# Reading the moving operands of split fp32 products from two alternating places

## The chip, the cores and the metric

The kernel runs on one core of one Trainium2 chip. The metric is the device time of one execution in microseconds. Three runs of the kernel before took 567.93, 568.34 and 568.43 us; their median is 568.34 us. A difference of some 0.2% (1.1 us) is about the least that can be told from none.

The core's engines appear in the profile as PE (TensorE matmuls), PEld (TensorE weight loads), DVE (VectorE), ACT (ScalarE), POOL (GpSimd) and SP (SyncE, which issues most DMAs). A TensorE matmul has a stationary operand, the weights, which are loaded into the array first, and a moving operand, whose columns stream through it one after another.

## The reference

The reference is a decoder trunk of two layers on one sequence of 256 tokens with a model width of 1024, all in float32:

```
for i in range(DEPTH):                       # 2 layers
    h = rmsnorm(x, norm_mix[i])
    x = x + rglru_mixer(h, ...)              # layer 0: recurrent block
    x = x + nsa_mixer(h, ...)                # layer 1: sparse attention, 16 heads
    h = rmsnorm(x, norm_ffn[i])
    u = relu(h @ w_up)                       # 1024 x 4096
    x = x + (u * u) @ w_down                 # 4096 x 1024
out = rmsnorm(x, norm_final)
```

The recurrent block projects to 2048 columns, convolves, gates (block-diagonal 256 x 256 matrices), scans along the tokens and projects back. The attention block projects to queries, six sets of keys and values, and gates, attends over compressed, selected and window keys, and projects back.

## The kernel before

Activations lie transposed: features on the 128 partitions, the 256 tokens along the free dimension, eight such chunks for a width of 1024. A weight matrix arrives in pieces of 128 x 1024 (eight 128 x 128 blocks), read in one order throughout.

For precision at a high matmul rate, each float32 operand is split in two float32r parts: a high part, which is the value rounded, and a low part, which is the difference. A product is then three matmuls: high by high, high by low, low by high. `mm3` (lines 317 to 320) issues them for one 128 x 128 weight block and one chunk of 256 token columns, into one PSUM bank. It serves all projections, both MLPs and both output projections. The weight block is the stationary operand, and the 256 activation columns (`hhl`, the split normed input; `uhl`, the split MLP hidden layer; `xbh`/`xbl`, the product of the recurrent block; `oh`/`ol`, the attention output) are the moving one. In `values` (line 993 on) it is the other way round: the activations are stationary and the weights move, in runs of 304 and 256 columns. The gates of the recurrent block (line 686), the score products (lines 1105 and 1106), the transposes (1159) and the attention's value products (1177) are not products of `mm3`.

The weight pieces are split on the device: ACT copies the high part (line 278 in the MLPs, the helper at line 326 elsewhere), and DVE subtracts to get the low part (287 and 323).

A finished bank is evicted by DVE, multiplied by the row `rs` that holds the norm's factor for each token: line 662 (convolution input), 723 (gelu branch), 778 (MLP hidden layer, with the relu), 887 (queries), 899 and 936 (keys, compressed inputs). In the MLP, ACT then squares the result twice, into a float32 `u` and into the float32r high part in `uhl` (783 and 784), and DVE writes the low part (785). Output projections and the MLP's second matmul are evicted by adding them to the residual `xt` (522). In attention, the output of `pv` is split out of its bank by the helpers at 326 (`copy`) and 323 (`diff`).

The two mixers are emitted by a planner (`Plan`): each piece of work is added with planned durations, the keys it reads and writes, and a due time; list scheduling with a few rounds of forward and backward passes gives one static order for each engine's queue. The MLPs are written out by hand: 32 hidden tiles of 24 matmuls each, then eight output tiles of 96, with `tick` placing the weight splits between them.

Of the kernel before, what the change touches and what calls it, by code (L numbers as in the profile page):

```python
# [219 lines left out]
def trunk_kernel(ctx: ExitStack, tc: tile.TileContext, x_in, vec_in, const_in, w2_in, wts, out):  # L220
# [71 lines left out]
    def later(fn):  # L292
        deferred.append(fn)
# [16 lines left out]
    def get(name, idx):  # L310
# [4 lines left out]
        return hi_t[i % NSPL], lo_t[i % NSPL]  # L315

    def mm3(ps, wh, wl, xh, xl, start, stop):
        pe.matmul(ps, wh, xh, start=start, stop=False)  # L318
        pe.matmul(ps, wh, xl, start=False, stop=False)  # L319
        pe.matmul(ps, wl, xh, start=False, stop=stop)  # L320
# [12 lines left out]
    class Section:  # L333
# [55 lines left out]
        def proj(self, name, idx, b, t, step, xs=None, xk=None):  # L389
            wh, wl, wk = self.weight(name, idx, t)  # L390
            z = self.bank((name, idx), b, zcols)
            xs, xk = xs or [(hh[:, k], hl[:, k]) for k in range(KC)], xk or hkey
            for i in range(0, 4, self.join):
                ks = range(2 * i, 2 * (i + self.join))

                def run(e, ks=ks):
                    for k in ks:
                        w = slice(k * P, (k + 1) * P)
                        mm3(z(), wh[:, w], wl[:, w], xs[k][0], xs[k][1], k == 0, k == KC - 1)
                self.add("pe", 0.68 * self.join, run, r=wk + list(xk[ks.start:ks.stop]), w=[("ps", b)], t=t + i * step)  # L400
            return z, ("ps", b)
# [72 lines left out]
    hhl = hpool.tile([P, KC, 2, S], F32R, name="hhl")  # L474
    hh, hl = hhl[:, :, 0], hhl[:, :, 1]
    acc = spool.tile([P, S], F32, name="acc")
    rs = spool.tile([P, S], F32, name="rstd")
# [47 lines left out]
    with ExitStack() as ph:  # L525
# [100 lines left out]
        xbh_b, xbl_b = (rg.tile([P, 8, S], F32R, name=n) for n in ("xbh", "xbl"))  # L626
        xb, r_t, i_t, y_t, t_t, xbh, xbl = ([x[:, m] for m in range(8)] for x in (xb_b, r_b, i_b, y_b, t_b, xbh_b, xbl_b))
        pair = lambda x, m: x[:, m // 2 * 2:m // 2 * 2 + 2]
# [15 lines left out]
        def conv(m, t):  # L644
            b = nextbank()
            if m < NFINE:
                wh, wl, _ = sec.weight("in", 8 + m, t)
                z, zk = sec.bank(("in", 8 + m), b, zcols), ("ps", b)
                for k in range(KC):
                    def run(e, k=k):  # L650
                        w = slice(k * P, (k + 1) * P)
                        mm3(z(), wh[:, w], wl[:, w], hh[:, k], hl[:, k], k == 0, k == KC - 1)
                        if m == 0 and k == 1:
                            keep_warm(8)
                    add("pe", 0.323 + 0.9 * (m == 0 and k == 1), run, r=[("hi0", m, k // 2), ("lo0", m, k // 2), ("hi", m), ("lo", m), hkey[k]],
                        w=[zk], t=m * 0.33 + k * NI * PJ / 2 if m < NI else t + k * PJ / 2)
            else:
                z, zk = sec.proj("in", 8 + m, b, t, PJ)
            t += 4 * PJ
            x, xk = xps[m % 3], ("xp", m % 3)  # L660
            bk = ("xb", m)
            add("dve", 0.34, lambda e: e.tensor_tensor(x[:, 3:], z(), rs, op=OP.mult), r=[zk, "rs"], w=[xk], t=t)
            add("act", 0.49, lambda e: e.activation(xb[m], x[:, 3:], AF.Identity, bias=col(V_CB, m), scale=cw(3, m)),
                r=[xk], w=[bk], t=t)
            for i in range(3):
                add("dve", 0.4, lambda e, i=i: e.scalar_tensor_tensor(xb[m], x[:, i:i + S], cw(i, m), xb[m], op0=OP.mult,
                                                                      op1=OP.add), r=[xk], w=[bk], t=t)
# [53 lines left out]
        def branch(m, t):  # L721
            z, zk = sec.proj("in", m, nextbank(), t, PJ)
            add("dve", 0.34, lambda e: e.tensor_tensor(y_t[m], z(), rs, op=OP.mult), r=[zk, "rs"], w=[("y", m)], t=t + 2.6)

        def product(m, t):
            yk, hk, lk = keys("y", m), keys("xbh", m), keys("xbl", m)
            y, h, l_, x = (pair(z, m) for z in (y_b, xbh_b, xbl_b, t_b))
            add("act", 0.53, lambda e: e.activation(y, y, AF.Gelu_apprx_tanh), r=["tab"], w=yk, t=t)
            add("dve", 0.6, lambda e: e.tensor_tensor(y, y, x, op=OP.mult), r=keys("t", m), w=yk, t=t)
            add(HI2, copy(h, y), r=yk, w=hk, t=t)  # L730
            add("dve", 0.6, diff(l_, y, h), r=yk + hk, w=lk, t=t)

# [33 lines left out]
    def mlp(layer, epilogue, first, last=None):  # L766
        with ExitStack() as ph:
# [4 lines left out]
            uhl = [up.tile([P, 2 * S], F32R, name="uhl", tag="uhl", bufs=NF) for _ in range(NF)]  # L772
            uh, ul = [x[:, :S] for x in uhl], [x[:, S:] for x in uhl]
            zrot = rotation(3, 4, 5, 0, 1, 2)

            def up_post(m, z):
                t = tmp.tile([P, S], F32, name="t", tag="t")
                dve.scalar_tensor_tensor(t, z, 0.0, rs, op0=OP.max, op1=OP.mult)  # L778
                flush()
                if m >= len(first) - 1:  # L780
                    tick(n=2 if m < 16 else 1)
                u = tmp.tile([P, S], F32, name="u", tag="u")
                act.activation(u, t, AF.Square)  # L783
                act.activation(uh[m], t, AF.Square)  # L784
                later(lambda: dve.tensor_tensor(ul[m], u, uh[m].bitcast(F32), op=OP.subtract))  # L785

            for m in range(NF):
                if m >= len(first):
                    z = next(zrot)[:, :S]
                    wh, wl = get("up%d" % layer, m)  # L790
                    for k in range(KC):
                        w = slice(k * P, (k + 1) * P)
                        mm3(z, wh[:, w], wl[:, w], hh[:, k], hl[:, k], k == 0, k == KC - 1)
                else:
                    z = first[m]()
                up_post(m, z)
# [29 lines left out]
    with ExitStack() as ph:  # L826
# [27 lines left out]
        oht, olt = (at.tile([P, 8 * S], F32R, name=n) for n in ("oh", "ol"))  # L854
        oh, ol = ([x[:, i * S:(i + 1) * S] for i in range(8)] for x in (oht, olt))
        NPT_ = 16
# [24 lines left out]
        def qchunk(c, b, t, step):  # L881
# [4 lines left out]
            ak, bk = ("sa", c % NQ), ("sb", c % NQ)  # L886
            add("dve", 0.4, lambda e: e.scalar_tensor_tensor(x, z(), cst[:, C_QS + c:C_QS + c + 1], rs,
                                                             op0=OP.mult, op1=OP.mult), r=[zk, "rs"], w=[xk], t=t)
# [6 lines left out]
        def kchunk(gp, br, b, t, step):  # L895
            z, zk = proj_t(("ks", "kw")[br], gp, b, t, step)
            t += 4 * step
            x, xk, l_, lk = turn()
            add("dve", 0.34, lambda e: e.tensor_tensor(x, z(), rs, op=OP.mult), r=[zk, "rs"], w=[xk], t=t)
            x, l_ = two_blocks(x), two_blocks(l_)  # L900
# [31 lines left out]
        def cproj(i, gp, b, t, step):  # L932
            z, zk = proj_t(("ck", "cv")[i], gp, b, t, step)
            t += 4 * step
            x, xk, _, _ = turn()
            add("dve", 0.34, lambda e: e.tensor_tensor(x, z(), rs, op=OP.mult), r=[zk, "rs"], w=[xk], t=t)
            for hf in range(2):
# [60 lines left out]
        def values(t):  # L998
# [3 lines left out]
            for i in range(4):  # L1002
                wh, wl, wk = weight("v", i, t + 2.8 * i)
                for kk in range(2):
                    k = 2 * i + kk
                    for h in range(2):
                        def run(e, wh=wh, wl=wl, k=k, kk=kk, h=h):
                            ts_ = slice(h * P, (h + 1) * P)
                            for b, c0 in enumerate((0, S + 48)):
                                ws = slice(kk * NVCOL + c0, kk * NVCOL + c0 + ncol[b])  # L1010
                                ps = vz[h][b]()
                                e.matmul(ps, hh[:, k, ts_], wh[:, ws], start=(k == 0), stop=False)  # L1012
                                e.matmul(ps, hh[:, k, ts_], wl[:, ws], start=False, stop=False)  # L1013
                                e.matmul(ps, hl[:, k, ts_], wh[:, ws], start=False, stop=(k == KC - 1))  # L1014
                        add("pe", 0.77, run, r=wk + [hkey[k]], w=[("ps", banks[h][0]), ("ps", banks[h][1])],
# [153 lines left out]
        def pv(js, t):  # L1169
            bk, n = [("ps", 7)], len(js)  # L1170
            o = zview(("o", js[0]), 7, lambda x: x[:, :n * S])
            cols = slice(js[0] * S, (js[-1] + 1) * S)

            def run(e):
# [14 lines left out]
            ok, lk = ([(x, j) for j in js] for x in ("oh", "ol"))  # L1189
            add([("act", 0.1 + 0.24 * n, 0.0), ("dve", 0.07 + 0.27 * n, 0.2)], lambda e: copy(oht[:, cols], o())(e), r=bk, w=ok,  # L1190
                t=t + 1.9 * n)
            add("dve", 0.07 + 0.27 * n, lambda e: diff(olt[:, cols], o(), oht[:, cols])(e), r=bk + ok, w=lk, t=t + 1.9 * n + 0.3)

# [115 lines left out]
def _arrange(inp):  # L1309
# [26 lines left out]
    kv = lambda i: win[:, D + i * S:D + (i + 1) * S]  # L1336
    wv = np.concatenate([kv(3), win[:, D + 6 * S:], kv(5)], axis=1).reshape(KC, P, NVCOL)
    wo = f["nsa_w_out"][0]
# [72 lines left out]
```

## Time and profile before

| | |
|---|---|
| median of three runs | 568.34 us |
| span of the profiled execution, first to last instruction | 566.4 us |
| median of the runs less that span | 1.9 us |
| mean granted TensorE clock | 0.997 |
| PE busy | 559.3 us, 4902 records |
| DVE busy | 407.6 us, 873 instructions |
| ACT busy | 343.9 us, 670 instructions |
| moved by DMA | 103.66 MB, mean 183 GB/s |

The profile shows one execution; its span stands for its own time, and the runs' times hold some 2 us more around it. Busy times of matmul records overlap: a record lasts longer than the distance to the next record's start, so the cost of a matmul is read from the distance of starts, or from counts in a window. In the views, a line such as "L318 PE MATMUL bank<-hhl,whi 128*128 128x256 f32" is line 318 of the kernel, on TensorE, writing `bank` from `hhl` and `whi`, with a 128 x 128 stationary operand and 256 moving columns.

### The profile page before, as it was taken

How to read it: one execution, taken by the hardware profiler on the slowest of the kernel's cores; microseconds unless marked ns; L12 is line 12 of the kernel's file. 1: busy time of each engine (PE TensorE's matmuls, PEld its weight loads, DVE VectorE, ACT ScalarE, POOL GpSimd, SP SyncE). 2: the span in 40 equal slices, each digit the busy share in tenths (PEclk: the TensorE clock that was granted, in tenths of full speed). 3: DMA queues.
4: the chain of work that ended last, by engine and by line, in shares of the span. 5: the costliest groups of instructions: out<-in, count | busy, mean ns of one | idle time of the engine just before them, and what ended most of it. 6: DMA issues, size and time to landing. Idle time of an engine off the chain costs nothing.

```text
span 566.4 us, 12406 instructions
## 1 busy us (share of the span) xinstructions
PE 559.3 (99%) x4902; PEld 552.9 (98%) x4902; DVE 407.6 (72%) x873; ACT 343.9 (61%) x670; POOL 40.1 (7%) x55
## 2 busy tenths in 40 slices
PE   9999999999999999999999999999999999999995
PEld 9989999999999999999999999999999999999995
DVE  6899989776676565466839999999767775563532
ACT  7699675866564443354647999875855664443421
POOL 1000000000000121131000000000000000222310
PEclk9999999999999999999999999999999999999998
DMA  8936467566667456555765431264766667566402
GB/s 319 407 91 220 117 219 247 176 204 192 188 192 249 155 189 217 190 181 175 276 188 166 140 99 57 75 224 138 221 200 192 196 200 233 154 202 221 132 1 74
DMA packets 33225, 103.66 MB, mean 183 GB/s; under 512 B 3856, under 2 KB 8080, under 8 KB 33168
## 3 DMA queue, kind: packets, MB, share of 16 engines
q1 hardware_dynamic: 32624, 102.42, 56.1%
q8 instruction: 38, 0.62, 0.5%
q10 hardware_dynamic: 544, 0.46, 0.2%
q14 instruction: 19, 0.16, 0.1%
HBM read 99.23 MB, written 1.05 MB: 177 GB/s over the span
## 4 chain that ended last, share of the span: by engine, by line
PE 99%; DVE 0%; ACT 0%; DVEq 0%; POOL 0%; issue 0%; POOLq 0%
PE bank L318 28%; PE bank L319 28%; PE bank L320 28%; PE bank L1177 3%; PE bank L686 2%; PE bank L1159 2%; PE bank L1105 1%; PE bank L1106 1%; PE bank L567 1%; PE bank L1012 1%; PE bank L1013 1%; PE bank L1014 1%; PE bank L953 1%; DVE xg L1295 0%; PE bank L1287 0%; DVEq L1406 0%
## 5 line engine op out<-in xcount | busy, mean ns | idle before, releaser
L318 PE MATMUL bank<-hhl,whi 128*128 128x256 f32 x768 | 213.1, 278 | 0.0
L319 PE MATMUL bank<-hhl,whi 128*128 128x256 f32 x768 | 212.4, 277 | 0.0
L320 PE MATMUL bank<-hhl,wlo 128*128 128x256 f32 x768 | 212.3, 276 | 0.0
L318 PEld LDWEIGHTS bank<-hhl,whi 128*128 128x128 f32 x768 | 144.5, 188 | 0.1
L287 DVE TENSOR_TENSOR wlo<-raw,whi 128x1024 fp32r<-128x1024 f32 x115 | 143.2, 1266 | 1.9 <-ACT whi L278 1.9
L319 PEld LDWEIGHTS bank<-hhl,whi 128*128 128x128 f32 x768 | 144.5, 188 | 0.1
L320 PEld LDWEIGHTS bank<-hhl,wlo 128*128 128x128 f32 x768 | 144.4, 188 | 0.0
L319 PE MATMUL bank<-uhl,whi 128*128 128x256 f32 x512 | 141.4, 276 | 0.0
L320 PE MATMUL bank<-uhl,wlo 128*128 128x256 f32 x512 | 141.3, 276 | 0.0
L318 PE MATMUL bank<-uhl,whi 128*128 128x256 f32 x512 | 141.3, 276 | 0.0
L278 ACT CAST whi<-raw 128x1024 fp32r<-128x1024 f32 x116 | 118.1, 1039 | 23.1 <-issue 18.8
L318 PEld LDWEIGHTS bank<-uhl,whi 128*128 128x128 f32 x512 | 96.1, 188 | 0.0
L320 PEld LDWEIGHTS bank<-uhl,wlo 128*128 128x128 f32 x512 | 96.1, 188 | 0.0
L319 PEld LDWEIGHTS bank<-uhl,whi 128*128 128x128 f32 x512 | 96.1, 188 | 0.0
L323 DVE TENSOR_TENSOR wlo<-raw,whi 128x1024 fp32r<-128x1024 f32 (+2 forms) x72 | 77.1, 1089 | 2.9 <-ACT whi L326 2.8
L326 ACT CAST whi<-raw 128x1024 fp32r<-128x1024 f32 (+2 forms) x64 | 61.2, 969 | 16.8 <-PE bank L319 7.8
L522 DVE TENSOR_TENSOR xt<-xt,bank 128x256 f32<-128x256 f32 x39 | 15.9, 417 | 74.8 <-PE bank L320 74.5
L783 ACT ACTIVATE u<-t 128x256 f32<-128x256 f32 x64 | 26.7, 418 | 58.6 <-DVE t L778 57.2
L778 DVE SCALAR_TENSOR_TENSOR t<-bank,rstd 128x256 f32<-128x256 f32 x64 | 26.9, 423 | 41.0 <-PE bank L320 40.7
L1119 ACT ACTIVATE pt<-pt,mx 128x128 f32<-128x128 f32 (+1 forms) x64 | 28.6, 450 | 1.8 <-DVE mx L1116 1.4
L785 DVE TENSOR_TENSOR uhl<-u,uhl 128x256 fp32r<-128x256 f32 x64 | 26.6, 416 | 3.0 <-ACT uhl L784 3.0
L498 ACT ACTIVATE hhl<-xt,vec 128x256 fp32r<-128x256 f32 x8 | 4.1, 510 | 39.4 <-DVE xt L522 39.4
(202 smaller groups left out, 732.6 us busy)
## 6 DMA issues: line engine op xcount, KB each, us to landing
raw<-in_dram SPq DMA_DIRECT2D x171, 512.0 KB, 4.4
raw<-in_dram SPq DMA_DIRECT2D x4, 560.0 KB, 4.6
gw<-in_dram SPq DMA_DIRECT2D x4, 512.0 KB, 8.9
raw<-in_dram SPq DMA_DIRECT2D x6, 256.0 KB, 4.9
y<-in_dram SPq DMA_DIRECT2D x2, 512.0 KB, 7.4
pT<-in_dram SPq DMA_DIRECT2D x2, 512.0 KB, 5.4
xt<-in_dram SPq DMA_DIRECT2D x3, 256.0 KB, 4.9
kl<-tl SPq DMA_DIRECT2D x8, 64.0 KB, 4.0
```

The costliest lines, as they stand in the source:

```text
L278: (act.copy if eng is None else eng.tensor_copy)(hi_t[i % NSPL][:, :n], raw_of(i)[:, :n])
L287: (eng or dve).tensor_tensor(lo[:, :n], raw_of(i)[:, :n], hi[:, :n].bitcast(F32), op=OP.subtract)
L318: pe.matmul(ps, wh, xh, start=start, stop=False)
L319: pe.matmul(ps, wh, xl, start=False, stop=False)
L320: pe.matmul(ps, wl, xh, start=False, stop=stop)
L323: return lambda e: e.tensor_tensor(o, a, h.bitcast(F32), op=OP.subtract)
L326: return lambda e: (e.copy if e is act else e.tensor_copy)(o, a)
L778: dve.scalar_tensor_tensor(t, z, 0.0, rs, op0=OP.max, op1=OP.mult)
L783: act.activation(u, t, AF.Square)
L785: later(lambda: dve.tensor_tensor(ul[m], u, uh[m].bitcast(F32), op=OP.subtract))
L1119: add("act", (0.39, 0.49)[qc], lambda e, row=row, j=j: e.activation(row, row, AF.Exp, bias=mx[:, j:j + 1], scale=-1.0, accum_out=sm[:, j:j ...
L1177: two = lambda c, w, y, **k: [e.matmul(o()[own_(hf), c0 + c.start:c0 + c.stop], w(hf), y(hf), **k) for hf in range(2)]
```

## The change

Three small helpers make views of a tile. `walk` shows 256 columns in the order 0, 128, 1, 129, ..., as pairs of columns 128 apart; `walks` does so for each chunk of a tile of several chunks; `pairs` shows columns in their plain order, two by two, so that its shape fits the others.

- In `mm3`, the destination in PSUM is viewed as `pairs`, which leaves its order as it was, and every caller hands in the moving operand as a `walk` view. The 256 columns of one matmul are thus read in turn from the first and the second half of the chunk.
- Where the moving operand holds tokens in their plain order (`hhl`), the result in PSUM has the tokens interleaved (token 0, 128, 1, ...). The eviction undoes it: it reads PSUM in order and writes its tile through `walk`, and reads `rs` through `walk`.
- Where the moving operand is itself written on the device for a later product (`uhl`, `xbh`/`xbl`, `oh`/`ol`), it is written through the `walk` view, so that the alternating read returns the tokens in plain order, and the residual addition at line 522 stays as it is.
- In `values`, the moving weights are read as `walk` views, for runs of 304 and 256 columns (152 and 128 apart), and the host stores these weight columns halved (all even ones, then all odd ones), so that the result comes out in plain order.

The number of instructions, their sizes, the planned durations and the DMAs are the same. The score products, gates, transposes and statistics keep their operands as they were.

```diff
+    def pairs(x):
+        return x.rearrange("p (a i) -> p a i", i=2)
+
+    def walk(x):
+        return x.rearrange("p (i a) -> p a i", i=2)
+
+    def walks(x):
+        return x.rearrange("p k (i a) -> p k a i", i=2)
+
     def mm3(ps, wh, wl, xh, xl, start, stop):
+        ps = pairs(ps)
         pe.matmul(ps, wh, xh, start=start, stop=False)
         pe.matmul(ps, wh, xl, start=False, stop=False)
         pe.matmul(ps, wl, xh, start=False, stop=stop)
...
-            xs, xk = xs or [(hh[:, k], hl[:, k]) for k in range(KC)], xk or hkey
+            xs, xk = xs or [(hhw[:, k], hlw[:, k]) for k in range(KC)], xk or hkey
...
     hh, hl = hhl[:, :, 0], hhl[:, :, 1]
+    hhw, hlw = walks(hh), walks(hl)
...
+        xbhw, xblw = walks(xbh_b), walks(xbl_b)
...
-            add("dve", 0.34, lambda e: e.tensor_tensor(x[:, 3:], z(), rs, op=OP.mult), r=[zk, "rs"], w=[xk], t=t)
+            add("dve", 0.34, lambda e: e.tensor_tensor(walk(x[:, 3:]), pairs(z()), walk(rs), op=OP.mult), r=[zk, "rs"], w=[xk], t=t)
...
-            y, h, l_, x = (pair(z, m) for z in (y_b, xbh_b, xbl_b, t_b))
+            y, h, l_, x = (pair(z, m) for z in (y_b, xbhw, xblw, t_b))
+            yw = y.rearrange("p k (a i) -> p k a i", i=2)
...
-            add(HI2, copy(h, y), r=yk, w=hk, t=t)
-            add("dve", 0.6, diff(l_, y, h), r=yk + hk, w=lk, t=t)
+            add(HI2, copy(h, yw), r=yk, w=hk, t=t)
+            add("dve", 0.6, diff(l_, yw, h), r=yk + hk, w=lk, t=t)
...
-            uh, ul = [x[:, :S] for x in uhl], [x[:, S:] for x in uhl]
+            uh, ul = [walk(x[:, :S]) for x in uhl], [walk(x[:, S:]) for x in uhl]
...
-                dve.scalar_tensor_tensor(t, z, 0.0, rs, op0=OP.max, op1=OP.mult)
+                dve.scalar_tensor_tensor(walk(t), pairs(z), 0.0, walk(rs), op0=OP.max, op1=OP.mult)
...
-                act.activation(uh[m], t, AF.Square)
-                later(lambda: dve.tensor_tensor(ul[m], u, uh[m].bitcast(F32), op=OP.subtract))
+                act.activation(uh[m], pairs(t), AF.Square)
+                later(lambda: dve.tensor_tensor(ul[m], pairs(u), uh[m].bitcast(F32), op=OP.subtract))
...
-                                ps = vz[h][b]()
-                                e.matmul(ps, hh[:, k, ts_], wh[:, ws], start=(k == 0), stop=False)
-                                e.matmul(ps, hh[:, k, ts_], wl[:, ws], start=False, stop=False)
-                                e.matmul(ps, hl[:, k, ts_], wh[:, ws], start=False, stop=(k == KC - 1))
+                                ps = pairs(vz[h][b]())
+                                e.matmul(ps, hh[:, k, ts_], walk(wh[:, ws]), start=(k == 0), stop=False)
+                                e.matmul(ps, hh[:, k, ts_], walk(wl[:, ws]), start=False, stop=False)
+                                e.matmul(ps, hl[:, k, ts_], walk(wh[:, ws]), start=False, stop=(k == KC - 1))
...
-            add([("act", 0.1 + 0.24 * n, 0.0), ("dve", 0.07 + 0.27 * n, 0.2)], lambda e: copy(oht[:, cols], o())(e), r=bk, w=ok,
+            add([("act", 0.1 + 0.24 * n, 0.0), ("dve", 0.07 + 0.27 * n, 0.2)], lambda e: copy(ohw[:, oj], ow())(e), r=bk, w=ok,
...
-            add("dve", 0.07 + 0.27 * n, lambda e: diff(olt[:, cols], o(), oht[:, cols])(e), r=bk + ok, w=lk, t=t + 1.9 * n + 0.3)
+            add("dve", 0.07 + 0.27 * n, lambda e: diff(olw[:, oj], ow(), ohw[:, oj])(e), r=bk + ok, w=lk, t=t + 1.9 * n + 0.3)
...
-    wv = np.concatenate([kv(3), win[:, D + 6 * S:], kv(5)], axis=1).reshape(KC, P, NVCOL)
+    halved = lambda w: w.reshape(D, -1, 2).transpose(0, 2, 1).reshape(D, -1)
+    wv = np.concatenate([kv(3), win[:, D + 6 * S:]], axis=1), kv(5)
+    wv = np.concatenate([halved(w) for w in wv], axis=1).reshape(KC, P, NVCOL)
```

The other evictions (lines 723, 887, 899 and 936), the attention output `oh`/`ol` and the callers of `mm3` are changed in the same manner.

More of the change, by code (lines that the diff above doesn't have):

```diff
@@ L626, in trunk_kernel @@
         xbh_b, xbl_b = (rg.tile([P, 8, S], F32R, name=n) for n in ("xbh", "xbl"))
-        xb, r_t, i_t, y_t, t_t, xbh, xbl = ([x[:, m] for m in range(8)] for x in (xb_b, r_b, i_b, y_b, t_b, xbh_b, xbl_b))
+        xbhw, xblw = walks(xbh_b), walks(xbl_b)
+        xb, r_t, i_t, y_t, t_t, xbh, xbl = ([x[:, m] for m in range(8)] for x in (xb_b, r_b, i_b, y_b, t_b, xbhw, xblw))
         pair = lambda x, m: x[:, m // 2 * 2:m // 2 * 2 + 2]
@@ L651, in run @@
                         w = slice(k * P, (k + 1) * P)
-                        mm3(z(), wh[:, w], wl[:, w], hh[:, k], hl[:, k], k == 0, k == KC - 1)
+                        mm3(z(), wh[:, w], wl[:, w], hhw[:, k], hlw[:, k], k == 0, k == KC - 1)
                         if m == 0 and k == 1:
@@ L722, in branch @@
             z, zk = sec.proj("in", m, nextbank(), t, PJ)
-            add("dve", 0.34, lambda e: e.tensor_tensor(y_t[m], z(), rs, op=OP.mult), r=[zk, "rs"], w=[("y", m)], t=t + 2.6)
+            add("dve", 0.34, lambda e: e.tensor_tensor(walk(y_t[m]), pairs(z()), walk(rs), op=OP.mult), r=[zk, "rs"], w=[("y", m)], t=t + 2.6)
         def product(m, t):
             yk, hk, lk = keys("y", m), keys("xbh", m), keys("xbl", m)
-            y, h, l_, x = (pair(z, m) for z in (y_b, xbh_b, xbl_b, t_b))
+            y, h, l_, x = (pair(z, m) for z in (y_b, xbhw, xblw, t_b))
+            yw = y.rearrange("p k (a i) -> p k a i", i=2)
             add("act", 0.53, lambda e: e.activation(y, y, AF.Gelu_apprx_tanh), r=["tab"], w=yk, t=t)
             add("dve", 0.6, lambda e: e.tensor_tensor(y, y, x, op=OP.mult), r=keys("t", m), w=yk, t=t)
-            add(HI2, copy(h, y), r=yk, w=hk, t=t)
-            add("dve", 0.6, diff(l_, y, h), r=yk + hk, w=lk, t=t)
+            add(HI2, copy(h, yw), r=yk, w=hk, t=t)
+            add("dve", 0.6, diff(l_, yw, h), r=yk + hk, w=lk, t=t)
         at_ = {}
@@ L792, in mlp @@
                         w = slice(k * P, (k + 1) * P)
-                        mm3(z, wh[:, w], wl[:, w], hh[:, k], hl[:, k], k == 0, k == KC - 1)
+                        mm3(z, wh[:, w], wl[:, w], hhw[:, k], hlw[:, k], k == 0, k == KC - 1)
                 else:
@@ L854, in trunk_kernel @@
         oht, olt = (at.tile([P, 8 * S], F32R, name=n) for n in ("oh", "ol"))
-        oh, ol = ([x[:, i * S:(i + 1) * S] for i in range(8)] for x in (oht, olt))
+        ohw, olw = (walks(x.rearrange("p (k s) -> p k s", s=S)) for x in (oht, olt))
+        oh, ol = ([x[:, i] for i in range(8)] for x in (ohw, olw))
         NPT_ = 16
@@ L886, in qchunk @@
             ak, bk = ("sa", c % NQ), ("sb", c % NQ)
-            add("dve", 0.4, lambda e: e.scalar_tensor_tensor(x, z(), cst[:, C_QS + c:C_QS + c + 1], rs,
+            add("dve", 0.4, lambda e: e.scalar_tensor_tensor(walk(x), pairs(z()), cst[:, C_QS + c:C_QS + c + 1], walk(rs),
                                                              op0=OP.mult, op1=OP.mult), r=[zk, "rs"], w=[xk], t=t)
@@ L898, in kchunk @@
             x, xk, l_, lk = turn()
-            add("dve", 0.34, lambda e: e.tensor_tensor(x, z(), rs, op=OP.mult), r=[zk, "rs"], w=[xk], t=t)
+            add("dve", 0.34, lambda e, x=x: e.tensor_tensor(walk(x), pairs(z()), walk(rs), op=OP.mult), r=[zk, "rs"], w=[xk], t=t)
             x, l_ = two_blocks(x), two_blocks(l_)
@@ L935, in cproj @@
             x, xk, _, _ = turn()
-            add("dve", 0.34, lambda e: e.tensor_tensor(x, z(), rs, op=OP.mult), r=[zk, "rs"], w=[xk], t=t)
+            add("dve", 0.34, lambda e, x=x: e.tensor_tensor(walk(x), pairs(z()), walk(rs), op=OP.mult), r=[zk, "rs"], w=[xk], t=t)
             for hf in range(2):
@@ L1171, in pv @@
             o = zview(("o", js[0]), 7, lambda x: x[:, :n * S])
-            cols = slice(js[0] * S, (js[-1] + 1) * S)
+            oj = slice(js[0], js[-1] + 1)
+            ow = lambda: o().rearrange("p (k a i) -> p k a i", k=n, i=2)
             def run(e):
```

## The prediction

> **What bounds the kernel now.** I read the page's busy shares and the chain of waits first, then what TensorE waits for.
>
> ```profile
> span 566.4 us, 12406 instructions
> PE 559.3 (99%) x4902; PEld 552.9 (98%) x4902; DVE 407.6 (72%) x873; ACT 343.9 (61%) x670; POOL 40.1 (7%) x55
> PE 99%; DVE 0%; ACT 0%; DVEq 0%; POOL 0%; issue 0%; POOLq 0%
> PE bank L567 <- POOL warm L562: 1.3, 1, 1.3
> PE bank L1281 <- ACT sqh L1278: 0.3, 1, 0.3
> ```
>
> TensorE is busy for 99% of the span, the chain that ends last is TensorE for 99%, and it waited for other engines for 1.6 us in all. So time can only move through what a matmul costs, unless another engine becomes too slow to feed it. Busy time does not say what a matmul costs, because records overlap: each lasts about 0.28 us and the next starts much earlier. The spacing of starts is the price. Here is the order of time in the first MLP:
>
> ```profile
> 120.15 0.28 PE L320 MATMUL bank<-hhl,wlo 128*128 128x256 f32 x1
> 120.27 0.28 PE L318 MATMUL bank<-hhl,whi 128*128 128x256 f32 x1
> 120.38 0.28 PE L319 MATMUL bank<-hhl,whi 128*128 128x256 f32 x1
> 120.49 0.28 PE L320 MATMUL bank<-hhl,wlo 128*128 128x256 f32 x1
> ```
>
> Three products of `mm3` take 0.34 us, 113 ns each. Two long stretches by window (columns: length, then busy time and count of PE, weight loads, DVE, ACT, POOL; granted clock; DMA share; GB/s) give it finely:
>
> ```profile
> 95.00:165.00 70.00, 70.00 (x620) 70.00 (x619) 50.91 (x82) 43.98 (x83) 0.00 (x0) 1.00 0.64 199
> 190.00:260.00 70.00, 70.00 (x620) 70.00 (x619) 38.87 (x38) 27.45 (x31) 14.01 (x12) 1.00 0.60 198
> ```
>
> 620 counted in 70 us, or about 618 spacings (records that only reach over an edge are counted too), is 113.3 ns. It is the same in both windows at a granted clock of 1.00, though DVE is busy 51 us in one and 39 in the other, and ACT 44 and 27. So the spacing is set inside TensorE and its own operand reads, not by the other engines' traffic.
>
> **Is 113.3 ns all array time?** Other matmuls of this trace say no. From the chain in order of time (start, length, count):
>
> ```profile
> 29.64 12.95 PE bank L686 x60
> 331.86 0.66 PE bank L1159 x6
> 284.14 3.62 PE bank L953 x64
> ```
>
> L686 (the gates) multiplies plain fp32: 60 records of 256 columns in 12.95 us, 215.8 ns each. L1159 (the transposes) takes 0.66/6 = 110 ns for 128 columns. Both draw a column about every 0.84 ns, with a weight load for each. `mm3` draws columns about twice as fast. Half of a gate record is 107.9 ns for 256 columns; the transpose, with the same number of 0.42 ns slots, is 110. I take 109 ns, an estimate between these, as what 256 columns would cost if drawing them at the double rate added nothing. So 113.3 holds about 4.3 ns that appears only at the double rate. Other split products pay more, in the value projection, where the weights are the moving operand, and for a while in the query projection:
>
> ```profile
> 280.53 0.28 PE L1012 MATMUL bank<-whi,hhl 128*128 128x256 f32 x1
> 280.89 0.30 PE L1012 MATMUL bank<-whi,hhl 128*128 128x304 f32 x1
> 281.31 0.28 PE L1012 MATMUL bank<-whi,hhl 128*128 128x256 f32 x1
> 281.66 0.30 PE L1012 MATMUL bank<-whi,hhl 128*128 128x304 f32 x1
> ```
> ```profile
> 333.10 0.28 PE L318 MATMUL bank<-hhl,whi 128*128 128x256 f32 x1
> 333.46 0.28 PE L318 MATMUL bank<-hhl,whi 128*128 128x256 f32 x1
> 333.81 0.28 PE L318 MATMUL bank<-hhl,whi 128*128 128x256 f32 x1
> ```
>
> Three 256-column products of `values` take 0.35 to 0.36 us, 117 to 120 ns each; three of 304 columns take 0.42, 140 ns. The second fence shows the very instructions of `mm3` at 0.71/6 = 118 ns. So the extra is not a constant of the instruction: it goes with how the two operand streams of TensorE, the moving columns and the weights of the next product, meet. What comes from where, and when, matters, and that is what the change alters.
>
> **The change part by part.**
>
> *Reading the moving operand* (`mm3`, `values`). No instruction is added or taken away, and planned durations and queue orders stay as they are: SP and POOL are not touched. Only the order of the addresses changes: column 0, 128, 1, 129 and so on in place of 0, 1, 2, 3. Counts by line in the two long stretches:
>
> ```profile
> 45.00:265.00 220.00, 178.18 (x646) 121.18 (x646) 1.00 0.60 194
> 375.00:560.00 185.00, 148.19 (x537) 100.66 (x537) 1.00 0.55 172
> ```
>
> These are the rows of L318; L319 and L320 alternate with it one for one, so they hold 3 x (646 + 537) = 3549 products at 113.3 ns. No row of this trace has this address pattern at the double rate, so its price is bounded from both sides. The low end is 107.9 ns (half a gate record): 3549 x 5.4 = 19.2 us saved. The high end comes from L953, whose moving columns lie 16 elements apart: 62 columns in 3.62/64 = 56.6 ns a record, and, since it writes the two halves of the array in turn, up to 113 ns a pair. That is 0.9 to 1.8 ns per scattered column, and it allows anything up to a fourfold spacing. Between ends so far apart I take 109 ns: the extra shows only where neighbouring columns are drawn at the double rate from one contiguous run, that run is what the change ends, and L953 shows scattered columns, at the half rate, running within a few per cent of the gates' 0.84 ns if its two halves run one after the other. Saved: 3549 x 4.3 = 15.3 us.
>
> [...]
>
> The remaining 192 + 307 + 166 = 665 products of `mm3` lie in the loading phase and the attention:
>
> ```profile
> 5.00:30.00 25.00, 18.14 (x64) 12.30 (x64) 1.00 0.98 381
> 265.00:330.00 65.00, 28.30 (x102) 18.98 (x101) 1.00 0.58 182
> 330.00:375.00 45.00, 15.67 (x56) 10.47 (x56) 1.00 0.31 90
> ```
>
> At 4.3 ns they would give 2.9 us. I count half, 1.5, because the first stretch is set by transfers too (DMA share 0.98) and DVE is nearly full in the attention. `values` has 96 products: 48 of 256 columns at about 118 ns and 48 of 304 at 140. At 109, and 109 x 304/256 = 129, they save 48 x 9 + 48 x 11 = 1.0 us.
>
> *The evictions and splits that now write or read with a step of 128.* Their count does not change. DVE rows:
>
> ```profile
> L323 DVE TENSOR_TENSOR wlo<-raw,whi 128x1024 fp32r<-128x1024 f32 x56 | 67.4, 1216 | 2.8 <-ACT whi L326 2.8
> L323 DVE TENSOR_TENSOR wlo<-raw,whi 128x256 fp32r<-128x256 f32 x12 | 4.6, 419 | 0.0
> L778 DVE SCALAR_TENSOR_TENSOR t<-bank,rstd 128x256 f32<-128x256 f32 x64 | 26.9, 423 | 41.0 <-PE bank L320 40.7
> L785 DVE TENSOR_TENSOR uhl<-u,uhl 128x256 fp32r<-128x256 f32 x64 | 26.6, 416 | 3.0 <-ACT uhl L784 3.0
> ```
>
> Two-input DVE work goes at (1216 - 419)/768 = 1.04 ns per element. If each stepped element cost a second such slot, an eviction of 256 columns would go from 0.42 to 0.69 us. The cover, by stage:
>
> ```profile
> 20.00:60.00 40.00, 40.00 (x296) 38.35 (x297) 38.92 (x80) 38.00 (x70) 2.17 (x7) 1.00 0.56 196
> 60.00:170.00 110.00, 110.00 (x971) 110.00 (x970) 87.55 (x143) 70.45 (x125) 0.00 (x0) 1.00 0.64 198
> 310.00:375.00 65.00, 65.00 (x622) 61.41 (x622) 63.07 (x326) 59.14 (x191) 0.00 (x0) 1.00 0.34 99
> 375.00:470.00 95.00, 95.00 (x841) 95.00 (x840) 72.84 (x123) 63.03 (x117) 0.00 (x0) 1.00 0.63 199
> ```
>
> Each MLP has 32 of L778 and 32 of L785, so 64 x 0.27 = 17 us more in the worst case, against 22 us of DVE idle time in each of those stages: hidden. In 20 to 60 DVE has only 1.1 us to spare against at most 16 projection evictions, 4.3 us; in 310 to 375 it has 1.9 us against 9 evictions and 4 double-length differences, 4.6 us. Without cover that is up to 3.2 + 2.7 = 6 us, and the next matmul to want the bank is what would be late. The low end is nothing: one element per slot whatever its address. A gain is excluded, as no element is left out. I take 1 us, near the low end, since these rows show DVE issuing at its plain one-element pace, without a faster mode that a step could switch off. ACT's stepped writes (the squares, the attention copies) have 40, 32 and 6 us of idle time in these stages.
>
> *The host's reordering of the value weights* changes no transfer size and no device work: nothing.
>
> **Sum.** -15.3 - 1.5 - 1.0 + 1 = -16.8 us on a span of 566.4, so 549.6. The runs' median of 568.34 is 1.9 us above the profiled span, which I leave as it is: 551.5 us. Everything behind a matmul follows it, and at 4% less per product the feeds still fit: one weight piece serves 24 products, now 2.72 us and then 2.62, against 1.22 us on DVE for the low part.
>
> **The rivals.**
>
> *The read order is indifferent.* The extra belongs to the weight stream, or to a rhythm of issue, and 113.3 stays. For it: the extreme regularity, 618 spacings per 70 us in stages of very different load. Against it: transposes and gates load weights too and show no such extra. Time: 568.3, up to 570 with some DVE cost.
>
> *The good rhythm is lost* (the other side). `mm3` at 113.3 is the best of the double-rate rows; the other rows at 256 columns stand at 117 to 120. If alternating reads meet the weight reads the way those do, every product costs about 118: 3549 x 4.7 = +16.7 us, and 585. It decides as soon as the spacing exceeds 113.3 by more than 0.3 ns, which is 1.1 us. For it: the same instructions do run at 118 in the query projection. Against it: the weights as moving operand are one contiguous run as well, so contiguity does not protect.
>
> *One fetch per column.* If a fetch serves several neighbouring columns at the double rate, an alternating read needs one per column and falls to the half rate that the gates show, 215.8 ns: 3549 x 102.5 = +364 us in the long stretches, and about +68 for the other 665 products: 1000 us. For it: every row at the double rate here reads a contiguous run, and the scattered one is at the half rate. Against it: nothing measured. [...]
>
> **How the numbers follow.** Chances: the forecast 0.62, indifferent 0.13, lost rhythm 0.14, one fetch per column 0.11. The forecast's own range is 548 (107.9 ns) to 560 (half the extra stays, or DVE's 6 us come out). The wide range must leave out at most 0.2: 548 to 586 takes in the first three and leaves out the last and the edges. A change within 0.2% (1.1 us) can't be told from none. Faster 0.62; the same 0.13; slower 0.14 + 0.11 = 0.25.
>
> **What would show it.** Right: starts of L318 to L320 at 109 ns, about 642 counted in a 70 us MLP window in place of 620; the value projection at 109 and 129; L778 and L785 near 0.42 us. Indifferent: 620 again. Lost rhythm: about 595. One fetch per column: about 326. If L778 or L785 stand at 0.69 us, the evictions cost what I set aside, and waits of PE for DVE should appear between 310 and 375. I am wrong if the spacing does not fall, or if TensorE starts to wait.

## The result, and the profile after

The changed kernel takes 565.1 us (median of four runs, 564.78 to 565.2) against 568.25 us before (four runs). The ratio is 0.9943, 95% interval 0.9929 to 0.9958: faster by 0.6%, about 3.2 us. The prediction was 551.5 us.

The page of the changed kernel, first lines and chain (before, TensorE held 99% of the chain):

```profile
span 563.4 us, 12407 instructions
PE 553.3 (98%) x4902; PEld 544.9 (97%) x4902; DVE 429.6 (76%) x873; ACT 358.0 (64%) x670; POOL 40.2 (7%) x55
PE 78%; DVE 15%; DMA 3%; ACT 2%; issue 1%; SPq 1%; POOL 0%; DVEq 0%; ACTq 0%; POOLq 0%
```

The span is 3.0 us shorter. TensorE is busy 6.0 us less, so 3.0 us of idle time are new, and DVE now holds 15% of the chain. DVE is busy 22.0 us more and ACT 14.1 us more with the same number of instructions. The two windows inside the first MLP (length, then busy time and count of PE, weight loads, DVE, ACT, POOL; granted clock, DMA share, GB/s):

```profile
95.00:165.00 70.00, 70.00 (x629) 70.00 (x628) 59.06 (x84) 49.93 (x83) 0.00 (x0) 1.00 0.65 203
190.00:260.00 70.00, 70.00 (x629) 70.00 (x628) 39.37 (x38) 27.46 (x31) 13.98 (x12) 1.00 0.61 203
```

Some 627 spacings in 70 us are 111.6 ns, where 618 were 113.3. By the trace's starts, taken to the nanosecond, 600 products in a row of the MLP average 111.67 ns, and 113.33 before; I write 111.7 from here on. The read did become faster, by 1.7 ns a product, not by 4.3. The value projection went near to where it was expected, from 140 and 118 ns to about 130 and 111 (129 and 109 were predicted). Its order of time:

```profile
289.78 0.29 PE L1027 MATMUL bank<-wlo,hhl 128*128 128x304 f32 x1
289.91 0.29 PE L1028 MATMUL bank<-whi,hhl 128*128 128x304 f32 x1
290.04 0.27 PE L1026 MATMUL bank<-whi,hhl 128*128 128x256 f32 x1
290.15 0.28 PE L1027 MATMUL bank<-wlo,hhl 128*128 128x256 f32 x1
290.26 0.28 PE L1028 MATMUL bank<-whi,hhl 128*128 128x256 f32 x1
290.38 0.29 PE L1026 MATMUL bank<-whi,hhl 128*128 128x304 f32 x1
```

290.04 less 289.78 is 0.26 us for two products of 304 columns; 290.38 less 290.04 is 0.34 us for three of 256. To the nanosecond, the starts lie 132, 129 and 129 ns apart for three of 304 and then 109, 112 and 112 for three of 256, over and over.

The groups of the stepped evictions and of the low part of the recurrent block's product (`xbl`; its row before stands last), and the waits of TensorE (line numbers are those of the changed file: 791, 797 and 798 were 778, 784 and 785; 333 was 323):

```profile
L791 DVE SCALAR_TENSOR_TENSOR t<-bank,rstd 128x256 f32<-128x256 f32 x64 | 39.4, 620 | 22.7 <-PE bank L330 22.6
L798 DVE TENSOR_TENSOR uhl<-u,uhl 128x256 fp32r<-128x256 f32 x64 | 40.9, 639 | 2.8 <-ACT uhl L797 2.8
L797 ACT ACTIVATE uhl<-t 128x256 fp32r<-128x256 f32 x64 | 42.5, 664 | 0.0
L333 DVE TENSOR_TENSOR xbl<-y,xbh 128x512 fp32r<-128x512 f32 x4 | 4.4, 1103 | 0.1
L323 DVE TENSOR_TENSOR xbl<-y,xbh 128x512 fp32r<-128x512 f32 x4 | 2.7, 673 | 0.0
```
```profile
PE bank L329 <- DVE xbl L333: 1.2, 2, 1.0
PE bank L329 <- DVE ol L333: 0.7, 1, 0.7
PE bank L328 <- ACT xbh L336: 0.4, 1, 0.4
```

A stepped eviction on DVE went from 0.42 to 0.62 to 0.64 us, ACT's stepped square from 0.40 to 0.66 us, and a low part of 512 columns from 0.67 to 1.10 us. TensorE now waits for `xbl` and for the low part of the attention output (`ol`), which it did not before.

### The profile page after: what moved, and what is told of

The parts are those of the page before. It is cut to its first block, busy times and chain, and to the rows that moved or that the text cites. A ratio compares the mean times of both kernels' runs of the same rounds, so it can differ in the third digit from the quotient of the medians.

```text
span 563.4 us, 12407 instructions
## 1 busy us (share of the span) xinstructions
PE 553.3 (98%) x4902; PEld 544.9 (97%) x4902; DVE 429.6 (76%) x873; ACT 358.0 (64%) x670; POOL 40.2 (7%) x55
## 4 chain that ended last, share of the span: by engine, by line
PE 78%; DVE 15%; DMA 3%; ACT 2%; issue 1%; SPq 1%; POOL 0%; DVEq 0%; ACTq 0%; POOLq 0%
PE bank L329 24%; PE bank L328 23%; PE bank L330 23%; DVE wlo L333 3%; DMA raw<-in_dram 2%; PE bank L1192 2%; DVE xb L678 1%; DVE pt L1130 1%; PE bank L1173 1%; DVE pt L1158 1%; DVE t L730 1%; SPq L547 1%; PE bank L1026 1%; PE bank L1027 1%; PE bank L1028 1%
## 5 line engine op out<-in xcount | busy, mean ns | idle before, releaser
L328 PEld LDWEIGHTS bank<-hhl,whi 128*128 128x128 f32 x768 | 147.7, 192 | 0.4 <-DVE tt L950 0.3
L330 PEld LDWEIGHTS bank<-hhl,wlo 128*128 128x128 f32 x768 | 147.7, 192 | 0.0
L329 PEld LDWEIGHTS bank<-hhl,whi 128*128 128x128 f32 x768 | 147.7, 192 | 0.0
L278 ACT CAST whi<-raw 128x1024 fp32r<-128x1024 f32 x116 | 120.2, 1057 | 21.1 <-issue 17.9
L329 PEld LDWEIGHTS bank<-uhl,whi 128*128 128x128 f32 x512 | 98.3, 192 | 0.0
L330 PEld LDWEIGHTS bank<-uhl,wlo 128*128 128x128 f32 x512 | 98.3, 192 | 0.0
L328 PEld LDWEIGHTS bank<-uhl,whi 128*128 128x128 f32 x512 | 98.3, 192 | 0.0
L791 DVE SCALAR_TENSOR_TENSOR t<-bank,rstd 128x256 f32<-128x256 f32 x64 | 39.4, 620 | 22.7 <-PE bank L330 22.6
L798 DVE TENSOR_TENSOR uhl<-u,uhl 128x256 fp32r<-128x256 f32 x64 | 40.9, 639 | 2.8 <-ACT uhl L797 2.8
L797 ACT ACTIVATE uhl<-t 128x256 fp32r<-128x256 f32 x64 | 42.5, 664 | 0.0
```

What stands on the lines that cost most here:

```text
L278: (act.copy if eng is None else eng.tensor_copy)(hi_t[i % NSPL][:, :n], raw_of(i)[:, :n])
L791: dve.scalar_tensor_tensor(walk(t), pairs(z), 0.0, walk(rs), op0=OP.max, op1=OP.mult)
L797: act.activation(uh[m], pairs(t), AF.Square)
L798: later(lambda: dve.tensor_tensor(ul[m], pairs(u), uh[m].bitcast(F32), op=OP.subtract))
```

## The experiments

Theory A: the alternating read saves what the spacing shows, and the stepped evictions give a good part of it back. Rival B: the evictions are harmless, and the new waits come only from TensorE running ahead.

### The read alone

```diff
 def mm3(ps, wh, wl, xh, xl, start, stop):
+    ps, xh, xl = seq(ps), alt(xh), alt(xl)   # alt: 0, 128, 1, 129, ...
```

`values` reads its weights the same way; nothing else changes, so results come out in another order.

> The kernel before with the alternating read alone: mm3 and values read their moving operand through walk, and every eviction, split and host layout stays as it was (so tokens and value columns come out interleaved where they should not). Theory A (the read saves 1.7 ns per product, from 113.3 to 111.7 ns, and the stepped evictions of the full change give about half of it back in waits): spacing 111.7 ns, values at 109 to 112 and 129 ns, DVE and ACT rows as before, no new waits of PE; 4224 x 1.65 ns + 0.8 us saved, about 560.5 us. Rival B (the waits seen after the change come from TensorE being faster, not from the evictions): 565 us, with the same waits.

Measured: 559.83 us, ratio 0.9857 (0.9843 to 0.9872). In the windows view:

```profile
95.00:165.00 70.00, 70.00 (x629) 70.00 (x629) 51.42 (x84) 44.47 (x84) 0.00 (x0) 1.00 0.64 201
190.00:260.00 70.00, 70.00 (x630) 70.00 (x629) 38.81 (x40) 27.79 (x32) 15.72 (x18) 1.00 0.59 196
```

The spacing is that of the full change with DVE and ACT loaded as before, and the waits for `xbl` and `ol` are gone (TensorE's waits come to 1.8 us, with 1.6 before). The read is worth 568.0 - 559.8 = 8.2 us. Rival B falls: TensorE is just as fast here and does not wait for either.

### The stepped evictions alone

```diff
 def mm3(ps, wh, wl, xh, xl, start, stop):
-    ps = pairs(ps)
+    ps = halves(ps)                       # plain order again:
+    xh, xl = xh.rearrange("p a i -> p i a"), xl.rearrange("p a i -> p i a")
```

`values` reads in plain order again too.

> The changed kernel with contiguous reads in mm3 and values, so that only the stepped evictions and splits are left (the tokens are then in a wrong order). Theory A: spacing 113.3 ns as before, L778/L785-like rows at 0.62 and 0.64 us, waits of PE around the recurrent block's product and in the attention; 2 to 4 us slower than before, 570 to 572 us. Rival B: no waits, 568 us.

Measured: 573.35 us, ratio 1.0092 (1.0075 to 1.0109), 5.4 us slower. The two largest new waits are those of the changed kernel, though the spacing is the old one:

```profile
PE bank L332 <- DVE xbl L336: 1.2, 2, 1.0
PE bank L332 <- DVE ol L336: 0.7, 1, 0.7
```
```profile
190.00:260.00 70.00, 70.00 (x620) 70.00 (x619) 41.39 (x40) 29.33 (x33) 14.12 (x13) 1.00 0.59 195
```

These waits sum to 1.9 us only, as they count moments when no matmul is in flight. The starts show the whole loss: set matmul by matmul beside the kernel before, this run falls behind by 0.2 us in the first 45 us, 2.3 us in the recurrent block's product, 0.3 us near 280 us and 1.8 us between 330 and 381 us, 4.7 us in all in the profiled executions. Between these places, in both MLPs, it loses nothing.

So -8.2 for the read and +5.4 for the evictions make -2.8 us, against -3.2 measured for both. That is where the gain went. A and B differed on this run too, and it went A's way, at more than A's 2 to 4 us.

### The same evictions with the loops swapped

```diff
-dve.scalar_tensor_tensor(walk(t), pairs(z), 0.0, walk(rs), ...)      # p a i: destination steps 512 bytes
+dve.scalar_tensor_tensor(halves(t), evens(z), 0.0, halves(rs), ...)  # p i a: source steps 8 bytes
```

Every stepped eviction and split is done so; which element goes where is unchanged.

> The changed kernel with the loops of every stepped eviction and split swapped: the destination in SBUF is written in its plain order (first half, then second half), and the source, PSUM or SBUF, is read with a step of two columns (8 bytes). Same result, same number of instructions. Theory A with the step of 512 bytes as the cause of the dear evictions: the rows return from 0.62-0.66 us to about 0.42 us, the waits go, 561 us. Rival: any step costs the same on DVE and ACT: rows stay at 0.62 us or more, 565 us.

Measured: 559.97 us, ratio 0.9859 (0.9843 to 0.9876), equal to the read alone. The groups:

```profile
L803 DVE SCALAR_TENSOR_TENSOR t<-bank,rstd 128x256 f32<-128x256 f32 x64 | 26.8, 421 | 37.1 <-PE bank L342 36.8
L810 DVE TENSOR_TENSOR uhl<-u,uhl 128x256 fp32r<-128x256 f32 x64 | 27.7, 432 | 3.3 <-ACT uhl L809 3.3
L809 ACT ACTIVATE uhl<-t 128x256 fp32r<-128x256 f32 x64 | 31.0, 485 | 0.0
```

The waits for `xbl` and `ol` are gone again. It was the step of 512 bytes in SBUF that cost, not stepping as such: a PSUM source read at every second column costs DVE nothing (0.42 us), an SBUF source 0.02 us on DVE and 0.08 on ACT. On ACT only the write had the long step. On DVE a second operand in SBUF was read with it as well, and no run separates that from the write. This kernel computes the same thing as the kernels before and after the change, and is faster than both.

### What bounds the product at 111.7 ns?

In the value projection after the change, 304 columns take about 129 ns, and that is 109 ns worth for 256. So the moving side can probably go faster than 111.7, and something else seems to hold `mm3`. Theory C: the load of 128 weight columns. Rival D: a rest of the moving side's extra. The edit is made to the kernel with swapped loops (559.97 us), and it leaves out 32 of the 128 output rows in every product that neither starts nor ends its group:

```diff
+    if not (start or stop):
+        ps, wh, wl = ps[:96], wh[:, :96], wl[:, :96]
```

> The kernel with swapped loops, in which every product of mm3 that neither starts nor ends its group loads only 96 of its 128 weight columns and writes 96 partitions; the work of the other 32 output rows is left out there. The 256 moving columns and their order stay. Theory C (at 111.7 ns the weight load of 128 columns is what bounds a product, the alternating read itself needs only 109): such products fall to 109 ns, in the MLP's second matmul nearly all of them; about 642 counted per 70 us there; about 552 us. Rival D (111.7 is what is left of the moving side's extra): spacing stays at 111.7 and the time at 560 us.

Measured, in one run beside one of before (568.08): 552.36 us. Windows, and a load of each size from the groups:

```profile
190.00:260.00 70.00, 70.00 (x642) 70.00 (x641) 41.89 (x44) 29.53 (x35) 16.32 (x18) 1.00 0.58 191
```
```profile
L342 PEld LDWEIGHTS bank<-uhl,whi 128*96 128x96 f32 x481 | 78.3, 163 | 0.0
L343 PEld LDWEIGHTS bank<-hhl,whi 128*128 128x128 f32 x192 | 36.8, 192 | 0.0
```

About 640 spacings in 70 us are 109.4 ns. With the moving operand untouched and a quarter fewer weight columns, the product falls to the 109 ns of the prediction, and D falls. The edit also writes a quarter fewer rows of PSUM, which by itself would leave a rival. The value projection of the changed kernel answers it, with all 128 columns and rows: of its three products of 256 columns, the first takes 109 ns and the next two 112. The first comes behind three of 304 columns, at 129 ns each, and its load starts 127 ns ahead of it; the loads of the next two start 107 and 109 ns ahead. (Why the first product of 304 takes 132 stays open.) So 109 ns is measured twice, with a smaller load and, at full size, where the load had started earlier. Both fit C; that at 111.7 ns the weight load is late is my reading of them.

### Can the weight load gain in the same way?

An alternating order of the stationary columns was not run. (From here on, a line is a name for addresses: an aligned group of 16 bytes, four columns.) Two plain steps were run, on the kernel with swapped loops, with the blocks woven on the host to keep the result:

```diff
+def block(w, k):
+    return w[:, :D].rearrange("p (j k) -> p k j", k=8)[:, k]       # step 32 bytes
+    # second run: pairs of blocks woven, step 8 bytes
```

> The kernel with swapped loops, in which the 128 columns of each weight block of mm3 are read with a step of 8 columns (32 bytes); the host weaves the blocks of a piece so that the result is the same. The first three pieces and the value weights keep their layout. If the weight load bounds at 111.7 ns and its extra comes, as on the moving side, from reading a contiguous run: 109 ns and about 550 us. [...] If it does not care: 111.7 ns and 560 us.

> The kernel with swapped loops, in which two neighbouring weight blocks of mm3 are woven column by column on the host and each is read with a step of 2 columns (8 bytes), two columns of every 16-byte line; same result; first three pieces and value weights as they were. If the weight load, which bounds at 111.7 ns, gains from touching each line less often in a row: down to 109 ns and 550 us. [...] If it does not care: 111.7 ns, 560 us.

Measured, one run each: 1090.41 us for 32 bytes (before: 568.08) and 591.07 us for 8 bytes (before: 567.82). The window of 95 to 165 us in each:

```profile
95.00:165.00 70.00, 70.00 (x293) 70.00 (x293) 31.14 (x49) 22.16 (x35) 0.00 (x0) 1.00 0.33 106
```
```profile
95.00:165.00 70.00, 70.00 (x589) 70.00 (x588) 49.02 (x78) 44.21 (x78) 0.00 (x0) 1.00 0.55 188
```

That is 240 and 119 ns a product, or 1.9 and 0.93 ns per weight column, against 0.87 contiguous. Of the three forms the contiguous block is the best, so 111.7 stands for 128 x 128 blocks until a better one is found. The product became dearer (240 and 119 ns against 111.7) with only the reading of its weights changed, as C says.

### What is it about the read order?

The first attempt was a read order that needs no change elsewhere, because PSUM is written in the same jumping order:

```diff
+    ps, xh, xl = walk(ps), walk(xh), walk(xl)   # "p (i b c) -> p b i c", i=2, c=2: runs of two
```

> The kernel before, with mm3 and values reading two neighbouring columns from the first half, then two from the second half, and so on, and writing them to PSUM in the same jumping order, so that the result lies in plain order and no eviction and no layout changes. Theory A, if runs of two columns are enough to take the extra off the read and PSUM takes jumps between runs of 8 bytes at full rate: 111.7 ns, 560.5 us. Rival (jumps in PSUM cost time, or runs of two keep the extra): 113.3 ns and 568 us, or a larger spacing and over 570 us.

Measured: 800.13 us, ratio 1.4086 (1.4065 to 1.4107). Its two parts alone:

> The kernel before, with mm3 and values reading runs of two neighbouring columns in turn from the first and the second half (0, 1, 128, 129, 2, 3), and PSUM written in plain order; evictions as before, so tokens and value columns come out in another order. It is the earlier run with jumps in PSUM (800 us) without the jumps. If PSUM's jumps made that one slow: 111.7 to 113.3 ns, 560 to 568 us. If the read of runs of two made it slow: about 167 ns and 800 us.

> The kernel before, with mm3 and values reading their moving columns in plain order and writing PSUM in jumping order, runs of two columns in turn to the first and the second half; evictions as before, so tokens and value columns come out in another order. If PSUM's jumps made the earlier run slow: about 167 ns and 800 us. If not: 113.3 ns and 568 us.

Measured: 799.93 us for the read of runs of two, 568.12 us for the jumps in PSUM (before: 567.82). The window of each, in this order:

```profile
95.00:165.00 70.00, 70.00 (x421) 70.00 (x420) 38.33 (x64) 32.33 (x58) 0.00 (x0) 1.00 0.36 122
```
```profile
95.00:165.00 70.00, 70.00 (x620) 70.00 (x619) 50.89 (x82) 44.24 (x83) 0.00 (x0) 1.00 0.60 199
```

167 ns against 113.3: it is the read, and PSUM takes jumps between runs of two columns for nothing. Reading 0, 1, 128, 129 takes half as long again as 0, 128, 1, 129. So more orders were read, by `mm3` alone (each as a comment with its view; the fourth and the fifth belong to the test at the end of this section):

```diff
+# 0, 16, 32, ... 240, 1, 17, ...    "p (q r) -> p r q", r=16
+# 0, 4, 1, 5, 2, 6, 3, 7, 8, 12     "p (b i a) -> p b a i", i=2, a=4
+# 0, 2, 1, 3, 4, 6, 5, 7            "p (b i a) -> p b a i", i=2, a=2
+# 0, 128, 2, 130, ... 1, 129, 3     "p (i a b) -> p b a i", i=2, b=2
+# 0, 64, 128, 192, 1, 65, ...       "p (i a) -> p a i", i=4
```

> The kernel before, with mm3 reading its 256 moving columns in turn from sixteen places 16 columns (64 bytes) apart: 0, 16, 32 and so on, then 1, 17; PSUM is written in order and evictions are as before, so tokens come out in another order; values is as before. If any read that leaves the 16-byte line at every column is as good as two places: 111.7 ns, 561 us. [...]

> The kernel before, with mm3 reading in turn from two places only 4 columns (16 bytes) apart: 0, 4, 1, 5, 2, 6, 3, 7, then 8, 12 and so on; PSUM in order, evictions as before, tokens in another order, values as before. If alternating between two neighbouring 16-byte lines is enough: 111.7 ns, 561 us. If the two places must lie far apart: 113.3 ns or more, 568 us or more.

> The kernel before, with mm3 reading its moving columns as 0, 2, 1, 3, then 4, 6, 5, 7: in turn from two places 2 columns (8 bytes) apart, within one 16-byte line; PSUM in order, evictions as before, tokens in another order, values as before. If what helps is that neighbouring columns come from two different lines: no gain, 113.3 ns and 568 us. If any break of the plain order helps: 111.7 ns, 561 us.

One run each. Sixteen places: 1018.68 us (before: 568.08). Two places 16 bytes apart: 560.85 us (568.08). Two places 8 bytes apart: 567.92 us (567.82). Their windows, in this order:

```profile
95.00:165.00 70.00, 70.00 (x321) 65.61 (x320) 33.23 (x52) 24.29 (x38) 0.00 (x0) 1.00 0.37 117
```
```profile
95.00:165.00 70.00, 70.00 (x630) 70.00 (x629) 51.43 (x84) 44.40 (x83) 0.00 (x0) 1.00 0.65 203
```
```profile
95.00:165.00 70.00, 70.00 (x620) 70.00 (x619) 50.89 (x82) 44.36 (x83) 0.00 (x0) 1.00 0.58 199
```

219, 111.7 and 113.3 ns. The distance of 128 columns is not needed, two neighbouring lines do. One count sorts all of these: take the even places of the order and the odd places apart, and count how many columns in a row of each lie in one line. In plain order there are two (0, 2, then 4, 6); alternating between two lines, four; alternating within a line, two; with runs of two or sixteen places, one. Two last orders set this count against the simpler rule that neighbours must come from different places (Model N):

> The kernel before, with mm3 reading in turn from two places 128 columns apart, but in each of them first all even columns, then all odd ones: 0, 128, 2, 130, 4, 132, and later 1, 129, 3, 131. PSUM in order, evictions as before, tokens in another order, values as before. [...] Model N (it is enough that neighbours in the order come from two different places): 111.7 ns and 561 us.

> The kernel before, with mm3 reading in turn from four places 64 columns apart: 0, 64, 128, 192, 1, 65 and so on. PSUM in order, evictions as before, tokens in another order, values as before. [...] Model N: 111.7 ns, 561 us.

Measured: 568.34 us for the first (before: 568.65) and 680.44 us for the second. Windows, in this order:

```profile
95.00:165.00 70.00, 70.00 (x620) 70.00 (x619) 50.91 (x82) 44.02 (x83) 0.00 (x0) 1.00 0.63 198
```
```profile
95.00:165.00 70.00, 70.00 (x501) 70.00 (x501) 45.39 (x74) 37.24 (x68) 0.00 (x0) 1.00 0.51 166
```

The first order alternates between places 512 bytes apart and gains nothing: 113.3 ns, like the other orders with a count of two; the simpler rule, which said 111.7, falls. The second has a count of one and is slow, which the simpler rule excluded, but at 140 ns, less than the 167 and 219 of the other two orders with that count. The three slow orders come back to the same lines after different numbers of columns and at different distances; what sets their order stays open. The count thus sorts all eight orders into fast (111.7), plain (113.3) and slow (140 to 219), and does not give the sizes among the slow. It was drawn from the first six of them and sorted the last two right; how the columns are fetched no run shows. What the runs show is that the order of the columns alone moves a product between 111.7 and 219 ns; why it does stays open.

## Why the prediction was right or wrong

**The bound and the direction.** Right, with the exception that the prediction named itself: the spacing fell, and another engine became too slow to feed TensorE at a few places. That the sum still came out faster is in part luck, since the evictions gave back two thirds of what the read saved.

**The low price of an alternating read.** The step that failed. "I take 109 ns" was the price of drawing 256 columns, and that number was good: 109.4 ns were measured where the load had 96 weight columns in place of 128, and the value projection stood at 129 for 304 columns. But a product is a read and a weight load, and I put the load at nothing: the transposes (110 ns with a load each) and the gates "load weights too and show no such extra". Their loads do not look like those of `mm3`. The weight loads of the kernel before, by the lines' own instructions and, for `mm3`, from the page's groups:

```profile
L1159 PEld LDWEIGHTS bank<-cst,pt x96: 137/141/143, 312.6 to 369.2; 128*128 128x128 f32 x96
L686 PEld LDWEIGHTS bank<-xb,gw x64: 187/190/191, 29.4 to 43.6; 128*128 128x128 f32 x64
```
```profile
L318 PEld LDWEIGHTS bank<-hhl,whi 128*128 128x128 f32 x768 | 144.5, 188 | 0.1
```

The record of a transpose's load lasts 141 ns, one of `mm3` 188, like a gate's. (Such records overlap, so they rank the loads and do not price them; no run here prices a transpose's load.) The gates have the long record, but one per 216 ns, which leaves it room to hide. No row of before showed such a load at the double rate without the moving side's extra, and I should have bounded it as a rival: the weight load takes over, at 111.7 ns. In the two long stretches the term was 3549 x 1.7 = 6 us, not 15.3.

The support that I drew from L953 does not hold either. Its condition was that the two halves run one after the other; by the trace's starts, the two records of a pair begin 9 ns apart and the pairs follow each other every 108 ns (medians), so the halves run together. A scattered column may thus have cost up to 1.7 ns, twice the gates' 0.84. That two alternating places are cheap was a guess that came true, and the sixteen places show how it could have failed.

**The remaining products and the value projection.** 1.5 and 1.0 us were taken. By the starts, the read alone saved 2.0 us in the remaining products and 0.8 in `values`, close to it, but partly by luck: 1.7 ns for each of 665 would have made 1.1. Those between 265 and 375 us had in part stood above 113.3 ns (118 in the query projection) and fell to 112 as well, 3.2 ns each on average.

**The stepped evictions.** The other mis-sized term. The worst case on record was 0.69 us per eviction and 6 us on the path, by the stages 20 to 60 and 310 to 375; measured were 0.62 to 0.64 us and 5.4 us. I took 1 us, arguing that DVE already works at its plain pace (1.04 ns per element, where its casts at line 326 took 683 ns for 1024 columns and 290 for 256, 0.51 ns per element). That says nothing of the SBUF side, and the swapped loops show that it was the 512-byte step there. The MLPs' cover held, as said: no wait for an MLP eviction appears among TensorE's waits. I looked for the waits between 310 and 375; one came in the recurrent block's product, from 66 to 73 us, which I had not listed because it lies outside 20 to 60, and another at 375.7. The first is the lack of cover in 20 to 60 come late: the chain that ends in it is DVE work with hardly a gap from 59.7 us on.

**The chances.** Indifference and a lost rhythm did not happen: two alternating places took 111.7 ns, not 113.3 or 118. Nor did one fetch per column, which was priced at 215.8 ns and 1000 us. Sixteen places did cost about that, 219 ns and 1018.68 us, but no run shows what is fetched when. Runs of two columns from each of two places took 167 ns, less than that price and more than the plain order.

**The sum.** -16.8 predicted; -8.2 + 5.4 = -2.8 by the parts; -3.2 measured. The forecast's own range, 548 to 560, did not hold the time. The wide one, 548 to 586, did, but it was drawn for rivals that did not happen, so that is luck.

## What to carry to other kernels

Before pricing one operand of a matmul, ask what the other one costs in the same time: a row bounds it only if its weight load is of the same kind and comes as often (here 109 ns was taken from rows with another load, and 111.7 came). When a layout must be permuted on the way out of PSUM, let the side that is read take the short step and write SBUF contiguously (an MLP eviction took 421 ns so, and 620 the other way); the same permutation cost 5.4 us or nothing measurable depending on which loop was inner. And an edit with two halves should be run in halves: read and evictions alone explained a result that looked like almost no effect.

## What the runs showed of the hardware that was not expected

- The order of the moving columns of a float32r product matters in both directions: 111.7 ns for 0, 128, 1, 129 and for 0, 4, 1, 5; 113.3 in plain order, for 0, 2, 1, 3 and for 0, 128, 2, 130; 140 for four places, 167 for runs of two from two places, 219 for sixteen (256 columns each, clock 1.00).
- With the moving columns read from two places in turn, a product with a 128 x 128 float32r weight block takes 111.7 ns; with 96 weight columns, and as many output rows, it takes 109.4.
- With a weight block read with a step, a product takes 119 ns at 8 bytes and 240 ns at 32 bytes, against 111.7 contiguous.
- PSUM written in runs of two columns that alternate between two halves costs nothing: 568.12 us against 567.82.
- Going back and forth between two places 512 bytes apart in SBUF costs a DVE instruction of 256 columns 0.2 us (423 to 620 ns and 416 to 639; written, and a second operand read) and an ACT one 0.26 us (403 to 664 ns; written); a source read 8 bytes apart costs 0 to 0.02 us on DVE (421 and 432 ns), and 0.08 us on ACT from SBUF (485 ns).
